# Softmax with a negated maximum and the scale moved out of the exponential, and the background modulation on VectorE alone, in a two-layer attention trunk

## The chip, the core and the metric

The kernel runs on one core of a Trainium2 chip. The metric is device time in microseconds (us), the median of several executions. The page of the profile and all queries below describe one execution on that core; their times count from the start of its span. Engines: PE multiplies matrices, PEld loads its weights, DVE is VectorE, ACT is ScalarE, POOL is GpSimd, SP issues the DMAs. Each engine works through its own queue in order, so an instruction that waits holds up all behind it on that engine.

## What is computed

512 latent tokens and 256 context tokens of width 2048 pass two layers. Each layer normalises its input, scales and shifts it with vectors made from a conditioning vector (the modulation), projects it, runs two kinds of attention, gates, projects back and adds. Cut to what matters:

```python
for l in range(2):
    mod  = silu(c)     @ w_mod[l] + b_mod[l]       # shift, scale, gate of the latents
    cmod = silu(c_ctx) @ w_mod[l] + b_mod[l]       # the same for the context
    h  = rmsnorm(x,  norm_g[l]) * (1 + scale)  + shift
    hc = rmsnorm(cx, norm_g[l]) * (1 + cscale) + cshift
    u, uc = h @ w_in, hc @ w_in
    # layer 0: A (8 heads) and B (8 heads);  layer 1: C (8 heads) and D (8 heads)
    y = concat(mixer1(u, uc), mixer2(u, uc)) * silu(ug)
    x = x + gate * (y @ w_o[l])                    # layer 0 does it for cx too

# A, differential:  p = softmax(q1 k1 / 8) - lam * softmax(q2 k2 / 8);  o = p v, then an RMS norm
# B, windowed:      p = softmax([s_ctx, s_window, sink])[..., :-1];      o = p v
# C and D:          p = softmax(scale * q k);                            o = p v
```

C has RMS-normalised queries and D low-rank ones, so the scale of a query row in C and D depends on the token.

## The kernel before, in words

**Precision.** Each fp32 operand of a matmul is split in a rounded high part and the rest, and a product is three matmuls (high by high, low by high, high by low). For each weight chunk ACT rounds (`wh`, L259) and DVE subtracts (`wl`, L218, a helper that all such subtractions share).

**Projections.** `proj` (L283) multiplies 16 chunks of the hidden state with one column block of weights, lines L278, L279 and L281, into PSUM banks `J`. ACT copies the result out: `r` for queries and keys (`roped`, L411 and L413, followed by the rotation with DVE L401 and L402 and POOL L403 and L404), `ev` for values (L447, L448).

**Attention.** For a block of 128 queries `scores` puts q k into the PSUM tile `S`, of which there is one. `softmax` (L484) takes on DVE the row maximum `mc` (L489), turns it into the bias `nb` (L492 with a sink, L494 without), on ACT the exponential `e` with its row sum `den` (L498), and on DVE the reciprocal `rd` (L503). The caller scales `e` by `rd` (L605 in B, L721 in C and D). In A the second map is multiplied by `r2` (L555) and added to the first times `r1` (L556). `p_transpose` transposes `e` on PE (L518) and splits it into `pth` (ACT L522) and `ptl` (DVE L218); `av` multiplies with the values (L533). In A and B the scale is an immediate number in the exponential and in `nb`; in C and D it is a column per query block, `qsc` or `dqs`, kept with both signs side by side (`both_signs`, L712).

**Modulation.** The shift and scale of layer 0 are made on PE at the start, up to about 170 us (`mod_first`). All others, 16 blocks of 512 columns, are made in the background by `mod_later` (L156): a block reads eight pieces of weights `mraw` (two buffers), and for each piece two rows `i` and the two vectors `v` (latents and context) it adds weight times a column of `silc` to `macc`. For `v = 0` DVE does multiply and add in one (L173). For `v = 1` ACT multiplies in place (L170) and POOL adds (L171). The last four blocks have `v = 0` alone.

**Order.** The program is one stream of instructions; the framework's scheduler sets each engine's order when it is built. `tick(n)` in the program counts up how many pieces of the modulation are due, so the pieces are handed over between heads: a few in A, most in B, the rest with the output projection. The stages by the time in the profile: layer 0's input up to about 220 us, A up to about 860, B up to 1370, output projection of layer 0 up to 1605, layer 1's input up to 1690, C up to 2140, D up to 2410, the end.

## Time and profile before

| what | value |
|---|---|
| median of 3 runs | 2575.29 us (2571.32 to 2575.84) |
| the profiled execution, its own time | 2573.45 us |
| its span in the profile | 2571.7 us |
| mean granted TensorE clock | 0.977 |
| PE busy | 2427.3 us, 94% |
| PEld busy | 2088.3 us, 81% |
| DVE busy | 1608.2 us, 63% |
| ACT busy | 1128.6 us, 44% |
| POOL busy | 517.6 us, 20% |

The profiled execution stands 0.07% under the median. A busy PE is not a PE at its peak, since matmuls are pipelined and their ends modelled; time that PE has lost shows as idle time in a stage and as a granted clock under 1.00. In a row of a window view the columns are the stretch, its length, the busy time of each engine with its instruction count, the granted clock, the busy share of the DMA engines and GB/s. In a row of a group they are line, engine, operation, tiles, shape and count, then busy us and mean ns, then the engine's idle time just before and what ended it. In a row of a timeline: start, duration, engine, line, operation, and in brackets idle time before it and what ended it.

### The profile page before, as it was taken

To read this page: it belongs to the slowest core of one execution; us is meant where nothing else is said; L and a number is where in the kernel's file an instruction comes from. 1 tells how busy PE (TensorE), PEld (TensorE's weight loads), DVE (VectorE), ACT (ScalarE), POOL (GpSimd) and SP (SyncE) were. 2 spreads that over 40 slices of the span, in tenths; PEclk is the share of its full clock that TensorE was granted. 3 is DMA by queue.
4 is the path that set the end of the run, shared out by engine and by line. 5 is a ranking of instruction groups with operands and counts; after the bars stand their busy time and mean duration, and the time that the engine had idled before them with its cause. 6 is when DMAs were issued, how large, how long until landed. Compare 5 with 4: busy or idle time off the path is not lost.

```text
span 2571.7 us, 36748 instructions
## 1 busy us (share of the span) xinstructions
PE 2427.3 (94%) x14214; PEld 2088.3 (81%) x14214; DVE 1608.2 (63%) x2720; ACT 1128.6 (44%) x2143; POOL 517.6 (20%) x340
## 2 busy tenths in 40 slices
PE   4889999999999999999999999899999999999998
PEld 2667888988788888878878888688888888887787
DVE  4367666656865787877666554857735325776534
ACT  3244444544554554544343332444434334554434
POOL 1132001101400354353303442310010001000010
PEclk9899999999999999999999999899999999999999
DMA  9762111111312233342334554535522222222234
GB/s 326 251 216 74 48 50 56 56 55 57 105 53 69 90 133 124 107 145 97 118 127 153 183 182 138 205 106 170 178 70 79 78 83 70 62 87 70 92 117 148
DMA packets 99087, 297.51 MB, mean 116 GB/s; under 512 B 11616, under 2 KB 12640, under 8 KB 98912
## 3 DMA queue, kind: packets, MB, share of 16 engines
q1 hardware_dynamic: 98912, 295.16, 34.5%
q8 instruction: 112, 1.84, 0.3%
q14 instruction: 63, 0.52, 0.1%
HBM read 269.16 MB, written 25.95 MB: 115 GB/s over the span
## 4 chain that ended last, share of the span: by engine, by line
PE 51%; DVE 7%; issue 2%; ACT 2%; DMA 2%; POOL 1%; ACTq 0%; SPq 0%; DVEq 0%; POOLq 0%
PE J L278 13%; PE J L279 13%; PE J L281 13%; PE O L533 4%; PE S L477 2%; DVE macc L173 2%; PE T L518 2%; DMA mraw<-in_wm_dram 2%; PE S L473 2%; DVE wl L218 1%; POOL macc L171 1%; DVE l L359 1%; DVE mc L489 1%; PE J L181 1%; PE T L243 0%
## 5 line engine op out<-in xcount | busy, mean ns | idle before, releaser
L278 PE MATMUL J<-h,wh 128*128 128x512 f32 (+1 forms) x2224 | 791.3, 359 | 23.8 <-ACT h L353 13.4
L279 PE MATMUL J<-l,wh 128*128 128x512 f32 (+1 forms) x2224 | 769.0, 356 | 4.7 <-DVE l L359 2.7
L281 PE MATMUL J<-h,wl 128*128 128x512 f32 (+1 forms) x2224 | 709.1, 356 | 2.8 <-DVE wl L218 2.8
L218 DVE TENSOR_TENSOR wl<-wraw,wh 128x512 fp32r<-128x512 f32 x500 | 402.2, 809 | 348.2 <-ACT wh L259 326.6
L259 ACT CAST wh<-wraw 128x512 fp32r<-128x512 f32 x492 | 302.4, 618 | 545.2 <-PE J L279 472.1
L278 PEld LDWEIGHTS J<-h,wh 128*128 128x128 f32 x2224 | 424.7, 192 | 104.7 <-ACT h L353 14.5
L279 PEld LDWEIGHTS J<-l,wh 128*128 128x128 f32 x2224 | 426.1, 192 | 62.6 <-DVE l L218 3.9
L281 PEld LDWEIGHTS J<-h,wl 128*128 128x128 f32 x2224 | 390.6, 192 | 38.8 <-DVE wl L218 5.1
L171 POOL TENSOR_TENSOR macc<-macc,mraw 128x512 f32<-128x512 f32 x180 | 267.9, 1489 | 254.1 <-ACT mraw L170 226.6
L278 PE MATMUL J<-yh,wh 128*128 128x512 f32 (+1 forms) x800 | 276.6, 352 | 5.1 <-ACT yh L441 5.1
L279 PE MATMUL J<-yl,wh 128*128 128x512 f32 (+1 forms) x800 | 272.8, 351 | 1.0 <-DVE yl L218 0.9
L173 DVE SCALAR_TENSOR_TENSOR macc<-mraw,silc,macc 128x512 f32<-128x512 f32 x240 | 241.7, 1007 | 42.3 <-DMA mraw<-in_wm_dram 38.6
L281 PE MATMUL J<-yh,wl 128*128 128x512 f32 (+1 forms) x800 | 253.2, 350 | 0.0
L489 DVE TENSOR_REDUCE mc<-S 128x1 f32<-128x768 f32 (+3 forms) x208 | 166.1, 799 | 137.9 <-PE S L477 88.1
L170 ACT ACTIVATE mraw<-mraw,silc 128x512 f32<-128x512 f32 x180 | 129.4, 723 | 192.4 <-DVE macc L173 171.6
L522 ACT CAST pth<-T 128x256 fp32r<-128x256 f32 (+2 forms) x288 | 124.9, 450 | 160.6 <-PE T L518 157.3
L278 PEld LDWEIGHTS J<-yh,wh 128*128 128x128 f32 x800 | 150.9, 190 | 32.8 <-ACT yh L441 5.9
L279 PEld LDWEIGHTS J<-yl,wh 128*128 128x128 f32 x800 | 151.1, 189 | 22.1 <-DVE yl L218 2.8
L218 DVE TENSOR_TENSOR ptl<-T,pth 128x256 fp32r<-128x256 f32 (+2 forms) x288 | 144.5, 514 | 38.6 <-ACT pth L522 35.1
L498 ACT ACTIVATE e<-S,nb 128x256 f32<-128x256 f32 (+3 forms) x144 | 104.3, 724 | 145.1 <-DVE nb L494 102.2
L281 PEld LDWEIGHTS J<-yh,wl 128*128 128x128 f32 x800 | 140.6, 190 | 12.4
L403 POOL TENSOR_TENSOR r<-r,cos 128x512 f32<-128x512 f32 x31 | 44.3, 1429 | 476.3 <-DVE t L402 361.4
(287 smaller groups left out, 3424.7 us busy)
## 6 DMA issues: line engine op xcount, KB each, us to landing
mraw<-in_wm_dram SPq DMA_DIRECT2D x128, 512.0 KB, 3.7
wraw<-in_ew_dram SPq DMA_DIRECT2D x96, 512.0 KB, 3.6
wraw<-in_ow_dram SPq DMA_DIRECT2D x64, 512.0 KB, 3.6
wraw<-in_wo_dram SPq DMA_DIRECT2D x62, 512.0 KB, 3.8
mraw<-in_wm_dram SPq DMA_DIRECT2D x80, 384.0 KB, 7.3
xT<-in_xT_dram SPq DMA_DIRECT2D x16, 384.0 KB, 7.8
res<-in_xT_dram SPq DMA_DIRECT2D x16, 384.0 KB, 4.4
xad<-nx SPq DMA_DIRECT2D x16, 384.0 KB, 2.3
```

Of the source, the lines that this page charges most:

```text
L170: nc.scalar.mul(rv[:, i, :], rv[:, i, :], sc)
L171: nc.gpsimd.tensor_tensor(macc[:, v, :], macc[:, v, :], rv[:, i, :], op=ALU.add)
L173: nc.vector.scalar_tensor_tensor(macc[:, v, :], rv[:, i, :], sc, macc[:, v, :], op0=ALU.mult, op1=ALU.add)
L218: nc.vector.tensor_tensor(o, a, h.bitcast(F32), op=ALU.subtract)
L259: nc.scalar.copy(wh[:, :n, :], rv[:, k0:k0 + n, :])
L278: nc.tensor.matmul(o, lhsT=wh, rhs=xh[:, c0:c1], start=first and (opens or o is lat), stop=False)
L279: nc.tensor.matmul(o, lhsT=wh, rhs=xl[:, c0:c1], start=False, stop=False)
L281: nc.tensor.matmul(o, lhsT=wl, rhs=xh[:, c0:c1], start=False, stop=last and (closes or o is lat))
L489: nc.vector.reduce_max(mc, S, axis=AX.X)
L498: nc.scalar.activation(e, S, AF.Exp, bias=nb, scale=scale, accum_out=den)
L522: nc.scalar.copy(ph, tv)
L533: nc.tensor.matmul(o, lhsT=v[:, cols[i]], rhs=pt[part][:, i, :], start=(n == 0), stop=(n == len(steps) - 1))
```

## The change

1. `softmax` lets the maximum come out negated (`tensor_reduce` with `negate=True`), so the multiplication by minus the scale goes. In A and B the scale is put into the queries where they leave PSUM (`roped`, L411 and L413: the copy becomes a multiplication), and the exponential's scale is 1. In C and D `nb` is multiplied by the scale column (`tensor_tensor`); with a sink, `nb` is the smaller of `nb` and `nsink` (`tensor_tensor` in place of `tensor_scalar`).
2. `both_signs` becomes `scaled`: one instruction in place of two, nine times.
3. The reciprocal moves out of `softmax` into `normed`. In A the first map is normed at once, before the second map's softmax; the second is then multiplied by `r2` and added to it in one instruction. The separate multiplication (L555) has gone from behind the second exponential.
4. In `mod_later` the branch for `v = 1` goes: 180 multiplications on ACT and 180 additions on POOL become 180 multiply-adds on DVE, as for `v = 0`.

```diff
@@ mod_later
                     if r == 0 and i == 0:
                         nc.scalar.mul(macc[:, v, :], rv[:, i, :], sc)
-                    elif v == 1:
-                        nc.scalar.mul(rv[:, i, :], rv[:, i, :], sc)
-                        nc.gpsimd.tensor_tensor(macc[:, v, :], macc[:, v, :], rv[:, i, :], op=ALU.add)
                     else:
                         nc.vector.scalar_tensor_tensor(macc[:, v, :], rv[:, i, :], sc, macc[:, v, :],
                                                        op0=ALU.mult, op1=ALU.add)
@@ roped
-    def roped(pl, pc, dim, mk=tmp):
+    def roped(pl, pc, dim, mk=tmp, scale=1.0):
         r = mk("r")
-        nc.scalar.copy(r[:, :512], pl)
+        nc.scalar.mul(r[:, :512], pl, scale)
...
@@ softmax
-    def softmax(S, scale, neg, sink=None):
+    def softmax(S, scale=None, sink=None):
         n = S.shape[-1]
-        mc = sm.tile([P, 1], F32, name="mc")
-        nc.vector.reduce_max(mc, S, axis=AX.X)
         nb = sm.tile([P, 1], F32, name="nb")
+        nc.vector.tensor_reduce(nb, S, axis=AX.X, op=ALU.max, negate=True)
+        if scale is not None:
+            nc.vector.tensor_tensor(nb, nb, scale, op=ALU.mult)
         if sink is not None:
-            nc.vector.tensor_scalar(nb, mc, neg, nsink[:, sink:sink + 1], op0=ALU.mult, op1=ALU.min)
-        else:
-            nc.vector.tensor_scalar(nb, mc, neg, None, op0=ALU.mult)
+            nc.vector.tensor_tensor(nb, nb, nsink[:, sink:sink + 1], op=ALU.min)
...
-        nc.scalar.activation(e, S, AF.Exp, bias=nb, scale=scale, accum_out=den)
+        nc.scalar.activation(e, S, AF.Exp, bias=nb, scale=1.0 if scale is None else scale, accum_out=den)
...
+        return e, den
+
+    def normed(e, den):
+        r = sm.tile([P, 1], F32, name="rd")
         nc.vector.reciprocal(r, den)
-        return e, r
+        nc.vector.tensor_scalar(e, e, r, None, op0=ALU.mult)
@@ a_attend
-                    e1, r1 = softmax(scores([(qa[:, c], k) for k in ka], lo, hi), 0.125, -0.125)
-                    e2, r2 = softmax(scores([(qb[:, c], k) for k in kb], lo, hi), 0.125, -0.125)
+                    e1, den = softmax(scores([(qa[:, c], k) for k in ka], lo, hi))
+                    normed(e1, den)
+                    e2, den = softmax(scores([(qb[:, c], k) for k in kb], lo, hi))
+                    r2 = sm.tile([P, 1], F32, name="rd")
+                    nc.vector.reciprocal(r2, den)
                     nc.vector.tensor_tensor(r2, r2, nlam, op=ALU.mult)
-                    nc.vector.tensor_scalar(e2, e2, r2, None, op0=ALU.mult)
-                    nc.vector.scalar_tensor_tensor(e1, e1, r1, e2, op0=ALU.mult, op1=ALU.add)
+                    nc.vector.scalar_tensor_tensor(e1, e2, r2, e1, op0=ALU.mult, op1=ALU.add)
@@ layer 1
-    def both_signs(cols, f):
...
+    def scaled(cols, f):
+        nc.vector.tensor_scalar(cols[:, :8], cols[:, :8], f, None, op0=ALU.mult)
```

In B and in C and D the callers do `e, den = softmax(...)` and `normed(e, den)` where they did the same work in one step before.

With the work, the scheduler's order moves on every engine. Lines of the changed kernel have other numbers (L170 is now the multiply-add, L486 the maximum, L490 the minimum with the sink, L497 the sum with the sink, L502 the reciprocal, L503 the scaling of `e`). Two places follow.

ACT, at the end of layer 0's input (190 to 215 us in the profile). Here `kh`, `qa`, `qb` and `vh` are rounded parts of A's first head, `th` is the gate, and `r` is the copy of the next head's key out of PSUM. Before:

```order
L433 CAST kh<-r 64x768 x2
L170 ACTIVATE mraw<-mraw,silc 128x512
L419 CAST qa<-r 64x768
L420 CAST qb<-r 64x768
L454 CAST vh<-J 128x512
L454 CAST vh<-J 128x256
L464 ACTIVATE th<-S 128x256
L170 ACTIVATE mraw<-mraw,silc 128x512
L411 COPY r<-J 128x512
```

And now:

```order
L430 CAST kh<-r 64x768 x2
L416 CAST qa<-r 64x768
L417 CAST qb<-r 64x768
L451 CAST vh<-J 128x512
L451 CAST vh<-J 128x256
L461 ACTIVATE th<-S 128x256
L408 ACTIVATE r<-J 128x512
```

The modulation's multiplications are gone from ACT's queue, and the copy `r`, which frees PE's bank, stands right behind `th`.

DVE, the first softmax of B (about 915 us in the profile); `ql` and `wl` are low parts of queries and weights. Before:

```order
L489 TENSOR_REDUCE mc<-S 128x1
L173 SCALAR_TENSOR_TENSOR macc<-mraw,silc,macc 128x512
L492 TENSOR_SCALAR nb<-mc,nsink 128x1
L173 SCALAR_TENSOR_TENSOR macc<-mraw,silc,macc 128x512
L502 TENSOR_TENSOR den<-den,es 128x1
L503 RECIPROCAL rd<-den 128x1
L605 TENSOR_SCALAR e<-e,rd 128x512
```

And now:

```order
L486 TENSOR_REDUCE nb<-S 128x1
L170 SCALAR_TENSOR_TENSOR macc<-mraw,silc,macc 128x512 x2
L490 TENSOR_TENSOR nb<-nb,nsink 128x1
L170 SCALAR_TENSOR_TENSOR macc<-mraw,silc,macc 128x512 x2
L215 TENSOR_TENSOR ql<-r,qh 128x768
L170 SCALAR_TENSOR_TENSOR macc<-mraw,silc,macc 128x512
L497 TENSOR_TENSOR den<-den,es 128x1
L170 SCALAR_TENSOR_TENSOR macc<-mraw,silc,macc 128x512
L215 TENSOR_TENSOR wl<-wraw,wh 128x512
L170 SCALAR_TENSOR_TENSOR macc<-mraw,silc,macc 128x512
L502 RECIPROCAL rd<-den 128x1
L170 SCALAR_TENSOR_TENSOR macc<-mraw,silc,macc 128x512 x2
```

Between the maximum and the scaled map stood two multiply-adds; nine stand there now (the scaling, L503, is the next row), and two subtractions.

More of the change, by code (lines that the diff above doesn't have):

```diff
@@ L407, in etile @@
         return sp["ep"].tile([P, TOK], F32, tag="e", name=name)
-    def roped(pl, pc, dim, mk=tmp):
+    def roped(pl, pc, dim, mk=tmp, scale=1.0):
         r = mk("r")
-        nc.scalar.copy(r[:, :512], pl)
+        nc.scalar.mul(r[:, :512], pl, scale)
         if pc is not None:
-            nc.scalar.copy(r[:, 512:768], pc)
+            nc.scalar.mul(r[:, 512:768], pc, scale)
         rope(r, dim)
@@ L579, in trunk_kernel @@
         tick(.4 if h else 0)
-        r = roped(*first(1, A_Q0), 64, mk)
+        r = roped(*first(1, A_Q0), 64, mk, 0.125)
         qa, qb = q_stacks(r, TOK, slotr)
@@ L603, in b_attend @@
             for u, h in enumerate(pr):
-                e, rd = softmax(scores(passes3(*qs[u], kh, kl, t), lo, hi, masks), SC128, -SC128, sink=h)
-                nc.vector.tensor_scalar(e, e, rd, None, op0=ALU.mult)
+                e, den = softmax(scores(passes3(*qs[u], kh, kl, t), lo, hi, masks), sink=h)
+                normed(e, den)
                 p_transpose(e, pt, u)
@@ L627, in trunk_kernel @@
             for h in pr:
-                r = roped(*proj(w, B_Q0 + 128 * h), 128)
+                r = roped(*proj(w, B_Q0 + 128 * h), 128, scale=SC128)
                 qs.append(split(r, TOK, slotr, "q"))
@@ L706, in trunk_kernel @@
             mm_step(lat, cx, ws4[i][k % 4], hT[k], k == 0, k == NCH - 1, opens=(i % 2 == 0), closes=(i % 2 == 1))
-    def both_signs(cols, f):
-        v = cols[:, :8].rearrange("p (t s) -> p t s", s=2)
-        for i, g in ((0, f), (1, -f)):
-            nc.vector.tensor_scalar(v[:, :, i], v[:, :, i], g, None, op0=ALU.mult)
+    def scaled(cols, f):
+        nc.vector.tensor_scalar(cols[:, :8], cols[:, :8], f, None, op0=ALU.mult)
     def full_attend(kfn, vh, vl, scale_of, sg=None):
@@ L719, in full_attend @@
                 t = 2 * pi + u
-                e, rd = softmax(scores(kfn(t), 0, 4), *scale_of(t))
-                nc.vector.tensor_scalar(e, e, rd, None, op0=ALU.mult)
+                e, den = softmax(scores(kfn(t), 0, 4), scale_of(t))
+                normed(e, den)
                 p_transpose(e, pt, u)
@@ L765, in d_lowrank @@
         cols = rstd_cols((acc,), range(4), 512, "dqs", tbank)
-        both_signs(cols, SC192)
+        scaled(cols, SC192)
         dqs.append(cols)
@@ L797, in trunk_kernel @@
             qsc = rstd_cols((sq,), range(4), P, "qsc", tbank)
-            both_signs(qsc, SC128)
+            scaled(qsc, SC128)
             rope(ev, 128)
@@ L801, in trunk_kernel @@
             o = full_attend(lambda t: passes3(qh, ql, kh, kl, t), vh, vl,
-                            lambda t: (qsc[:, 2 * t:2 * t + 1], qsc[:, 2 * t + 1:2 * t + 2]))
+                            lambda t: qsc[:, 2 * t:2 * t + 1])
             sg = silu2(*proj(w, O_G0 + 128 * h, lat_only=True), sgslot)
@@ L891, in trunk_kernel @@
             nc.sync.dma_start(sg[:, :512], sgd[h])
-            o = full_attend(passes, *vs[u], lambda t: (dqs[0][:, 2 * t:2 * t + 1], dqs[0][:, 2 * t + 1:2 * t + 2]), sg)
+            o = full_attend(passes, *vs[u], lambda t: dqs[0][:, 2 * t:2 * t + 1], sg)
             if h < 6:
```

1 line of the change is left out of this document (removed).

## The prediction

> **What bounds the kernel now.** I read the page's busy times, a table by stage, the list of waits, and the timeline where PE stood longest.
>
> ```profile
> PE 2427.3 (94%) x14214; PEld 2088.3 (81%) x14214; DVE 1608.2 (63%) x2720; ACT 1128.6 (44%) x2143; POOL 517.6 (20%) x340
> ```
>
> ```profile
> 150.00:220.00 70.00, 56.19 (x349) 43.92 (x348) 59.36 (x66) 35.90 (x58) 32.00 (x20) 0.93 0.45 144
> 220.00:640.00 420.00, 412.58 (x2538) 367.46 (x2537) 260.64 (x522) 199.50 (x383) 34.85 (x24) 1.00 0.16 54
> 640.00:700.00 60.00, 53.72 (x318) 47.53 (x317) 53.83 (x74) 33.54 (x58) 29.06 (x19) 0.94 0.35 115
> ...
> 860.00:1290.00 430.00, 403.65 (x2467) 357.57 (x2466) 325.82 (x490) 209.06 (x457) 196.09 (x130) 0.98 0.38 121
> ...
> 1370.00:1605.00 235.00, 235.00 (x1376) 207.37 (x1375) 138.67 (x158) 79.68 (x121) 93.81 (x59) 1.00 0.51 171
> ...
> 2140.00:2410.00 270.00, 256.24 (x1524) 218.65 (x1522) 188.03 (x362) 133.51 (x269) 14.47 (x11) 0.99 0.22 69
> ```
>
> PE bounds. What it loses in a stage is its idle time plus the share of the clock not granted. The two-vector modulation runs in four stretches: 150 to 220 loses 13.8 + 0.07 x 70 = 18.7 us, 640 to 700 loses 6.3 + 3.6 = 9.9, 860 to 1290 loses 26.4 + 8.6 = 35.0, and 1370 to 1605 nothing. Together that is 63.6 us. The same attention A without it, 220 to 640, loses 7.4 us in 420. So the modulation's neighbourhood is where PE starves, though no engine is full there: in 860 to 1290 DVE is busy 76%. A queue in order is one reason:
>
> ```profile
> ACT mraw L170 <- DVE macc L173: 171.6, 109, 4.7
> ...
> DVE macc L173 <- DMA mraw<-in_wm_dram: 38.6, 35, 3.1
> ```
>
> ```profile
> 1110.15 0.52 PE L281 MATMUL J<-h,wl 128*128 128x512 f32 x2
> 1111.63 1.75 DVE L173 SCALAR_TENSOR_TENSOR macc<-mraw,silc,macc 128x512 f32<-128x512 f32 x2 [0.71 <-DMA mraw<-in_wm_dram]
> ...
> 1112.68 1.46 ACT L170 ACTIVATE mraw<-mraw,silc 128x512 f32<-128x512 f32 x2 [2.70 <-DVE macc L173]
> ...
> 1114.87 0.59 ACT L447 COPY ev<-J 128x512 f32<-128x512 f32 x1
> ...
> 1115.52 0.90 PE L453 MATMUL J<-identr,ev 128*128 128x128 f32 x3 [4.85 <-ACT ev L447]
> ```
>
> ACT multiplies in place, so it waits until DVE has read the row; ACT stands 2.70 us behind DVE, which stood behind a DMA, and the copy `ev` that PE needs is queued behind ACT's multiplications. PE stands 4.85 us. The second reason is POOL. While it adds (first row), DVE's instructions take longer; after 691 they don't:
>
> ```profile
> 675.66 4.50 POOL L171 TENSOR_TENSOR macc<-macc,mraw 128x512 f32<-128x512 f32 x3
> ```
>
> ```profile
> 675.65 1.85 DVE L173 SCALAR_TENSOR_TENSOR macc<-mraw,silc,macc 128x512 f32<-128x512 f32 x1
> 677.43 1.62 DVE L555 TENSOR_SCALAR e<-e,rd 128x768 f32<-128x768 f32 x1
> 678.96 1.75 DVE L173 SCALAR_TENSOR_TENSOR macc<-mraw,silc,macc 128x512 f32<-128x512 f32 x1
> ...
> 691.16 0.16 DVE L554 TENSOR_TENSOR rd<-rd,nlam 128x1 f32<-128x1 f32 x1
> 691.35 0.62 DVE L555 TENSOR_SCALAR e<-e,rd 128x768 f32<-128x768 f32 x1
> ```
>
> ```profile
> 682.56 1.54 PE L518 MATMUL T<-identr,e 128*128 128x128 f32 x6 [5.20 <-DVE e L556]
> ```
>
> **The change part by part: DVE's load.** L173 alone, by stage, then POOL's L171 in 860 to 1290:
>
> ```profile
> 860.00:1290.00 430.00, 114.72 (x105) 0.98 0.38 121
> ...
> 1690.00:2140.00 450.00, 33.57 (x45) 1.00 0.33 107
> ```
>
> ```profile
> 860.00:1290.00 430.00, 155.38 (x105) 0.98 0.38 121
> ```
>
> Beside POOL's additions a multiply-add takes 114.72 / 105 = 1.093 us, without them 33.57 / 45 = 0.746. The 105 that move in this stage therefore cost 78 us, and the 105 already there give back 36. The rest gives back too; groups of 860 to 1290:
>
> ```profile
> L218 DVE TENSOR_TENSOR wl<-wraw,wh 128x512 fp32r<-128x512 f32 x72 | 76.1, 1062 | 38.5 <-ACT wh L259 33.6 <-PE J L281 3.7 <-PE J L279 0.6
> L605 DVE TENSOR_SCALAR e<-e,rd 128x512 f32<-128x512 f32 (+2 forms) x36 | 27.8, 774 | 0.9
> ...
> L502 DVE TENSOR_TENSOR den<-den,es 128x1 f32<-128x1 f32 x36 | 15.0, 417 | 14.0 <-ACT es L501 13.9
> ...
> L492 DVE TENSOR_SCALAR nb<-mc,nsink 128x1 f32<-128x1 f32 x36 | 7.5, 208 | 0.6
> ```
>
> L502 is L554's kind, 0.16 us when clean: 36 x 0.26 = 9. For `wl`, 0.746 is an upper bound (less work than a multiply-add): 72 x 0.32 = 23. L605 is at most 0.62 when clean (the longer L555): at least 36 x 0.15 = 6. That is 74 of 78 us, so DVE stays about as busy as now (bounds: +42 us if only L173 gains, -10 if the remaining small rows gain likewise), while ACT loses 180 instructions and POOL its 180 additions. I take zero net, nearest to the rows.
>
> **What PE gets back.** What ended its idle time in 860 to 1290, by group:
>
> ```profile
> L518 PE MATMUL T<-identr,e 128*128 128x128 f32 x144 | 23.4, 285 | 9.1 <-DVE e L605 9.1
> ...
> L473 PE MATMUL S<-kh,qh 128*128 128x256 f32 x36 | 11.4, 315 | 7.0 <-ACT e L498 3.4 <-ACT qh L441 3.3
> ...
> L453 PE MATMUL J<-identr,ev 128*128 128x128 f32 x12 | 2.4, 356 | 5.0 <-ACT ev L447 5.0
> ```
>
> Without L170 the copy `ev` starts at about 1112: 3 us of the 5.0. Of the 9.1 and 7.0 I take half, 8 us, since these waits hold both inflated DVE rows, which go, and multiply-adds queued ahead, which grow. Of the clock's 8.6 us half goes with the long stops: 4.3. With 0.9 behind POOL's last addition that is 16 us of 35.0; bounds are 4 (`ev` and the addition alone) and 35. In 640 to 700 the three DVE rows beside POOL's addition are 1.10 + 1.00 + 1.00 = 3.1 us too long, just before a stop of 5.20: 3 us, and half of the clock's 3.6, so 5 (bounds 0 and 9.9). In 150 to 220:
>
> ```profile
> 205.98 0.40 ACT L464 ACTIVATE th<-S 128x256 f32<-128x256 f32 x1
> 209.27 0.72 ACT L170 ACTIVATE mraw<-mraw,silc 128x512 f32<-128x512 f32 x1 [2.89 <-DVE macc L173]
> ```
>
> ```profile
> 210.52 0.58 PE L278 MATMUL J<-h,wh 128*128 128x256 f32 x1 [5.71 <-ACT r L411]
> ```
>
> The copy `r` now follows `th` at 206.4, not L170 at 209.9: 3.5 us, and 1.5 of the clock. Against it, 15 more multiply-adds, 11 us, stand between the subtractions for the last four hidden chunks; the 15 already there give back 4.8. I charge 2 us. Net 3 (bounds -4 and 18.7). In 1370 to 1605 PE is full: zero, covered by 96 us of idle DVE. SP issues the same DMAs; its `mraw` loads, with weight loads behind them, now wait for DVE alone. Landing takes 3.7 us and a piece 4 x 0.746 = 3.0 on DVE, so with two buffers DVE can wait 0.7 us or more per piece: zero if other rows stand between, 96 x 0.7 = 67 us if none do. I leave the 38.6 us as they are.
>
> ```profile
> mraw<-in_wm_dram SPq DMA_DIRECT2D x128, 512.0 KB, 3.7
> ```
>
> **The softmax edits.**
>
> ```profile
> L494 DVE TENSOR_SCALAR nb<-mc 128x1 f32<-128x1 f32 x96 | 14.2, 148 | 1.7
> ...
> L494 DVE TENSOR_SCALAR nb<-mc,dqs 128x1 f32<-128x1 f32 x32 | 6.6, 206 | 0.3
> ```
>
> A loses 96 x 0.148 = 14.2 us of DVE and gets the multiplication of the second map off the end of its chain; the cover is PE's queue of projections, full in 220 to 640, so 1 us shows (bounds 0 and 7.4). In D (2140 to 2410, PE idle 13.8) the 206 ns become a `tensor_tensor`, 0.16 when clean: 32 x 0.05 = 1.5, of which 1. A negating maximum I price as the old one; its price isn't in the trace, between zero and the 0.148 that it replaces. The nine fewer `scaled` rows, and ACT's copies turned into multiplications, are off the path: zero. B swaps the form of `nb`. The Trainium skill, "SBUF — State Buffer", "Who interferes with whom", says that a VectorE instruction with two inputs in SBUF contends with a GpSimd one that reads SBUF, and one with a single SBUF input outside the two-port modes does not. L502's 417 ns against L554's 0.16 us agrees. By that rule alone the new `nb` would pay L502's 0.26 us, 36 x 0.26 = 9 us, on the chain; with POOL busy 196.09 - 155.38 = 41 us there in place of 196, it is 2, about what the 208 ns of L492 give back.
>
> **The sum.** 16 + 5 + 3 + 2 = 26 us against the profiled execution's own 2573.45: 2547.4. That execution lies 1.8 us under the median of the runs, so I predict 2549.
>
> **Rivals.** (a) All the lost time in the four stretches returns, as in A without modulation: 63.6 less 2% of 795 us of stretches (16) and plus 2 is 50, so 2525; if nothing at all were lost there, 2510. For it: ACT's and POOL's share in every long stop. Against it: DVE's 76%. (b) The change doesn't do what it says: DVE's queue takes the place of ACT's, stops move but stay, 2573 within 5. The Trainium skill, "Perfetto Trace Analysis", "Optimizing Scalar/DVE Operations", says that work moved between GpSimd and VectorE might not help since they share a port; the slow rows agree on the sharing. (c) Slower: in B the multiply-adds lengthen the chain from maximum to scaled map. In the order quoted there are nine where two stood, 7 x 0.746 = 5.2 us more against about 1.2 us of inflation gone (2 x 0.35, 0.26, 0.15). Now PE waits (9.1 + 7.0) / 36 = 0.45 us per softmax. If that grows by 1 us, 36 us come on and only `ev`, the clock and the other stretches, about 16, go: 2595. It decides from about 0.45 us more per softmax. Against it: the same rows are DVE work that PE's projections cover today.
>
> **Chances.** The forecast 0.58, with its own range 2532 to 2564; (a) 0.15; (b) 0.12; (c) 0.15. About 0.2%, 5 us, is what a measurement can tell from no change. Faster takes the forecast, (a) and a quarter of (b): 0.76; same the rest of (b): 0.09; slower (c): 0.15. The range 2515 to 2583 leaves out part of (a) and most of (c).
>
> **What would show it.** The multiply-add (then L170) at about 0.75 us in every stage; no wait of ACT for it; ACT near 1128.6 - 180 x 0.73 = 997 us busy and POOL near 517.6 - 180 x 1.48 = 251, DVE within 40 of 1608; PE's loss in B (860 to 1290) near 19 us. Wrong: waits of PE for the scaled `e` or of ACT for `nb` in B above 16 us, or DVE waiting for `mraw` well over 38.6.

## The result: 2515.59 us, 0.9774 of the time before

| kernel | median | ratio to before, 95% interval |
|---|---|---|
| before | 2574.18 us (2571.32 to 2575.84, 4 runs) | 1 |
| after | 2515.59 us (2510.88 to 2520.86, 4 runs) | 0.9774 [0.9752, 0.9796] |

The change gains 58.6 us, where 26 were forecast: the direction is right, the time lies at the very lower end of the range 2515 to 2583 and below the forecast's own range 2532 to 2564, and the forecast gain is less than half of what came. The profiled execution of after has a span of 2508.9 us, 62.8 less than before's. The page's busy times, after:

```profile
PE 2408.6 (96%) x14214; PEld 2077.9 (83%) x14214; DVE 1574.6 (63%) x2795; ACT 1011.5 (40%) x1963; POOL 248.9 (10%) x160
```

PE is busy 18.7 us less for the same matmuls (they run at a higher granted clock, 0.985 for 0.977), and the other 44 us are idle time gone. DVE does the additions that POOL did, with 75 instructions more, and yet is busy 33.6 us less. The table by stage shows where PE's time came back. These are the stretches of the prediction, moved to where the same work lies in after; first the profile of after, then attention B alone (from its first query product to the first product of the output projection) in before:

```profile
150.00:208.00 58.00, 51.51 (x323) 40.19 (x323) 51.95 (x77) 24.95 (x42) 6.69 (x4) 0.94 0.46 157
640.00:700.00 60.00, 59.75 (x367) 53.07 (x366) 53.76 (x83) 26.93 (x51) 6.01 (x4) 1.00 0.32 106
889.00:1237.00 348.00, 345.83 (x2182) 311.28 (x2181) 271.24 (x536) 126.69 (x324) 36.50 (x22) 1.00 0.40 131
1310.00:1546.00 236.00, 236.00 (x1382) 208.35 (x1381) 137.33 (x203) 50.45 (x77) 27.00 (x14) 1.00 0.50 170
2140.00:2335.00 195.00, 189.94 (x1160) 163.08 (x1159) 140.91 (x282) 100.27 (x205) 8.01 (x6) 1.00 0.23 73
```

```profile
913.00:1293.00 380.00, 356.67 (x2176) 316.33 (x2175) 283.28 (x445) 184.81 (x414) 168.04 (x112) 0.97 0.38 121
```

B takes 348 us for 380. PE's loss there (idle time plus the clock's share) goes from 23.3 + 0.03 x 380 = 34.7 us to 2.2, while DVE is as full as before: 271 of 348 is 78%, 283 of 380 was 75%. DVE does 91 instructions more in B in 12 us less, because most of them are shorter. Groups of B in after (889 to 1237):

```profile
L170 DVE SCALAR_TENSOR_TENSOR macc<-mraw,silc,macc 128x512 f32<-128x512 f32 x180 | 133.3, 775 | 3.3 <-DMA mraw<-in_wm_dram 2.9 <-ACT macc L168 0.2
L215 DVE TENSOR_TENSOR wl<-wraw,wh 128x512 fp32r<-128x512 f32 x64 | 45.0, 703 | 34.6 <-ACT wh L256 33.3 <-PE J L278 1.0
...
L497 DVE TENSOR_TENSOR den<-den,es 128x1 f32<-128x1 f32 x36 | 5.6, 157 | 14.1 <-ACT es L496 14.1
```

The multiply-add is 0.74 us of busy time (133.3 / 180) where it was 1.09, `wl` 0.70 where it was 1.06, and the sum of two columns `den` 0.157 where it was 0.417.

Stages in us, each from one profiled execution, by landmarks in PE's rows: the start up to A's first query product; A; B up to the first product of the output projection; that projection (with B's last attention in it); layer 1's input; C; D up to its last query product. The last column is the median. The kernels are told below:

| kernel | start | A | B | out | input 1 | C | D | median |
|---|---|---|---|---|---|---|---|---|
| before | 216 | 697 | 380 | 313 | 85 | 506 | 200 | 2574 |
| mod_only | 212 | 695 | 350 | 312 | 85 | 506 | 200 | 2537 |
| act_dve | 206 | 695 | 350 | 312 | 89 | 505 | 201 | 2534 |
| pool_ts | 203 | 706 | 443 | 315 | 83 | 507 | 200 | 2633 |
| softmax_only | 216 | 690 | 388 | 310 | 91 | 505 | 195 | 2568 |
| after | 208 | 681 | 348 | 309 | 88 | 506 | 195 | 2516 |
| late_norm | 205 | 685 | 348 | 313 | 85 | 506 | 195 | 2513 |
| extra_nb | 206 | 689 | 348 | 310 | 89 | 505 | 195 | 2518 |
| both_back | 209 | 695 | 347 | 312 | 87 | 505 | 195 | 2526 |
| junk_b | 208 | 684 | 351 | 313 | 88 | 507 | 196 | 2522 |
| junk_b2 | 207 | 683 | 383 | 325 | 87 | 508 | 195 | 2564 |
| junk_b4 | 210 | 683 | 434 | 331 | 85 | 506 | 196 | 2618 |
| xn_dve | 209 | 684 | 348 | 311 | 75 | 507 | 195 | 2500 |
| after_rev | 208 | 686 | 347 | 310 | 88 | 505 | 196 | 2516 |
| all_dve | 215 | 684 | 347 | 309 | 77 | 505 | 199 | 2513 |

Between kernels that are alike there, the start varies by 5 us (205 to 210), input 1 by 8 (83 to 91 in all but xn_dve and all_dve) and A by 5 (681 to 686 in the six kernels that have after's A).

### The profile page after: what moved, and what is told of

The parts are those of the page before. It is cut to its first block, busy times and chain, and to the rows that moved or that the text cites. A ratio compares the mean times of both kernels' runs of the same rounds, so it can differ in the third digit from the quotient of the medians.

```text
span 2508.9 us, 36275 instructions
## 1 busy us (share of the span) xinstructions
PE 2408.6 (96%) x14214; PEld 2077.9 (83%) x14214; DVE 1574.6 (63%) x2795; ACT 1011.5 (40%) x1963; POOL 248.9 (10%) x160
## 3 DMA queue, kind: packets, MB, share of 16 engines
q1 hardware_dynamic: 98912, 295.16, 34.7%
## 4 chain that ended last, share of the span: by engine, by line
PE 88%; DVE 5%; DMA 3%; issue 2%; ACT 1%; SPq 0%; ACTq 0%; DVEq 0%
PE J L275 22%; PE J L276 22%; PE J L278 22%; PE O L532 6%; PE S L474 4%; PE T L517 3%; PE S L470 3%; DMA mraw<-in_wm_dram 2%; DVE macc L170 1%; PE T L144 1%; PE J L178 1%; DVE l L356 1%; DVE wl L215 1%; PE T L240 1%; PE T L220 1%
## 5 line engine op out<-in xcount | busy, mean ns | idle before, releaser
L275 PE MATMUL J<-h,wh 128*128 128x512 f32 (+1 forms) x2224 | 786.0, 357 | 18.7 <-ACT h L350 11.8
L215 DVE TENSOR_TENSOR wl<-wraw,wh 128x512 fp32r<-128x512 f32 x500 | 362.6, 729 | 338.7 <-ACT wh L256 325.2
L170 DVE SCALAR_TENSOR_TENSOR macc<-mraw,silc,macc 128x512 f32<-128x512 f32 x420 | 319.7, 792 | 28.6 <-DMA mraw<-in_wm_dram 26.2
L486 DVE TENSOR_REDUCE nb<-S 128x1 f32<-128x768 f32 (+3 forms) x208 | 166.2, 799 | 146.8 <-PE S L474 79.2
L517 PE MATMUL T<-identr,e 128*128 128x128 f32 x784 | 115.5, 274 | 2.9 <-DVE e L503 2.6
L517 PEld LDWEIGHTS T<-identr,e 128*128 128x128 f32 x784 | 94.6, 141 | 16.6 <-issue 2.6
```

Of the source, the lines that this page charges most:

```text
L170: nc.vector.scalar_tensor_tensor(macc[:, v, :], rv[:, i, :], sc, macc[:, v, :], op0=ALU.mult, op1=ALU.add)
L215: nc.vector.tensor_tensor(o, a, h.bitcast(F32), op=ALU.subtract)
L275: nc.tensor.matmul(o, lhsT=wh, rhs=xh[:, c0:c1], start=first and (opens or o is lat), stop=False)
L486: nc.vector.tensor_reduce(nb, S, axis=AX.X, op=ALU.max, negate=True)
L517: nc.tensor.transpose(out=tp[:, 128 * (b - b0):128 * (b - b0) + 128], in_=e[:, 128 * b:128 * b + 128], identity=ident)
```

## The experiments

Two theories stood at the start. P: POOL's additions lengthen DVE's instructions, through something that the two engines share, and DVE's instructions stand on the chain that PE waits for. Q: ACT, waiting in its queue for DVE's reads, holds up the copies and exponentials that PE needs.

### One part of the change each

**mod_only** is before with the branch of the second vector deleted, nothing else of the change:

```diff
-                    elif v == 1:
-                        nc.scalar.mul(rv[:, i, :], rv[:, i, :], sc)
-                        nc.gpsimd.tensor_tensor(macc[:, v, :], macc[:, v, :], rv[:, i, :], op=ALU.add)
```

> The kernel before with the modulation's v = 1 on VectorE and nothing else changed. Theory M (all of the gain comes from the modulation leaving ACT and POOL): about 2520 us, 54 less than before, and PE loses almost nothing from 860 to 1235 us. Theory S (the softmax edits bring a third or more, since chains with fewer steps hide the multiply-adds): about 2540 us, and B still loses 15 us. Theory O (the scheduler's new order was lucky, and no single part carries it): anywhere from 2530 to 2580.

Measured: 2537.17 us, 0.9856 [0.9841, 0.9871], 36.4 us gained.

**softmax_only** is after with these three lines put back.

> The changed kernel with the modulation put back on ACT and POOL as before. Theory M: 2570 us, within 6 of before, and B loses about 35 us as before. Theory S: 2550 us or less. Theory O: anywhere from 2540 to 2590.

Measured: 2568.46 us, 0.9978 [0.9966, 0.9991], 5.1 us gained. The parts alone give 36.4 + 5.1 = 41.5 of 58.6 us; behind the modulation's move the softmax edits give 2537.17 - 2515.59 = 21.6. The table shows where the 17 us more that come together lie: beside POOL's additions the new softmax makes B 8 us longer (388 for 380) and A 7 shorter, without them B 2 shorter and A 14. Groups by form, whole kernel, first softmax_only, then after:

```profile
L493 DVE TENSOR_TENSOR nb<-nb,nsink 128x1 f32<-128x1 f32 x48 | 18.3, 382 | 0.8
```

```profile
L490 DVE TENSOR_TENSOR nb<-nb,nsink 128x1 f32<-128x1 f32 x48 | 10.1, 211 | 0.7
```

The new form of `nb`, a `tensor_tensor` of two columns, takes 382 ns in a kernel with POOL's additions, for the 208 of the old form: 48 x 0.174 = 8.4 us, all on the chain between maximum and exponential. The prediction had 9 us for this price and saw it go with the additions; it did. The longest row of the old form in before is 0.216 us, that of the new form in softmax_only 1.248. The Trainium skill, "SBUF — State Buffer", "Who interferes with whom", names two SBUF inputs as what makes a VectorE instruction contend with a GpSimd one that reads SBUF, and excepts an instruction with one such input outside the two-port modes. By that rule the old form, if it ran in no such mode, would stay short and the new would not, and both rows agree. One input alone is no safe sign: the scaling of `e` has one tile as input too, and took 1.62 us for 0.62 in the rows of the prediction.

### P against Q

**act_dve** is before with POOL's additions on DVE; ACT still multiplies in place, and still waits:

```diff
-                        nc.gpsimd.tensor_tensor(macc[:, v, :], macc[:, v, :], rv[:, i, :], op=ALU.add)
+                        nc.vector.tensor_tensor(macc[:, v, :], macc[:, v, :], rv[:, i, :], op=ALU.add)
```

> The kernel before, with POOL's additions of the modulation moved to VectorE, while ACT still multiplies in place and so still waits for VectorE's reading. No POOL work beside it any more. Theory P (the shared reading port was the main cost): 2530 us, and a multiply-add takes 0.75 us. Theory Q (ACT's queue was the main cost, since the copies that PE needs stand behind multiplications that wait): 2560 us, with ACT's wait for the multiply-add still near 170 us and PE stopped behind ACT's copies.

Measured: 2534.28 us, 0.9841 [0.9826, 0.9856], 39.3 us gained. From the waits of ACT in act_dve, and its row for B:

```profile
ACT mraw L170 <- DVE macc L173: 134.5, 102, 4.2
```

```profile
901.00:1251.00 350.00, 345.41 (x2175) 310.27 (x2173) 271.69 (x535) 185.76 (x414) 36.36 (x22) 1.00 0.40 130
```

ACT does all its 180 multiplications and waits 134.5 us for DVE (171.6 in before), yet B is as short as in mod_only (350). PE's wait for the copy `ev`, 4.8 us of B in before, is not among its waits in B any more.

**pool_ts** is before with ACT's multiplications on POOL, so that ACT is free of the modulation and POOL does both steps:

```diff
-                        nc.scalar.mul(rv[:, i, :], rv[:, i, :], sc)
+                        nc.gpsimd.tensor_scalar(rv[:, i, :], rv[:, i, :], sc, None, op0=ALU.mult)
```

> The kernel before, with ACT's multiplication of the modulation moved to POOL (a tensor_scalar in place), so ACT is out of it and POOL has 360 instructions in place of 180. Theory Q: 2535 us, since no copy stands behind a waiting multiplication. Theory P: 2575 us or more, since POOL holds the port for longer and a multiply-add stays at 1.1 us or above in B.

Measured: 2633.18 us, 1.0228 [1.0211, 1.0245], 59.6 us lost. The row for B and the group of POOL's multiplications in pool_ts:

```profile
909.00:1352.00 443.00, 370.56 (x2193) 327.81 (x2191) 278.46 (x454) 129.54 (x328) 343.62 (x215) 0.90 0.34 109
```

```profile
L170 POOL TENSOR_SCALAR mraw<-mraw,silc 128x512 f32<-128x512 f32 x180 | 338.4, 1889 | 155.7 <-DVE macc L173 118.5 <-DVE nb L494 22.7 <-DVE modc L129 9.6
```

ACT has what Q wanted for it, and B grows by 63 us. Not all of that is sharing. POOL is busy 344 of 443 us in B, and PE waits 25.5 us for the modulation itself, which now comes late (in all, number of times, longest):

```profile
PE J L181 <- DVE macc L173: 25.5, 5, 10.7
```

So pool_ts shows that freeing ACT doesn't pay for more work on POOL, but not how much of the loss is the slowing of DVE. Q as the main cost falls by act_dve: ACT's wait was there, and in single places PE stood behind it, but the gain comes with 134.5 of its 171.6 us still there.

### POOL's additions with nobody waiting for them

Deleting POOL's additions also takes a dependence away. So they were given back to after as work that no one needs.

**junk_pool** adds four 128x128 additions into a scratch tile beside each multiply-add of the second vector:

```diff
+                        for _ in range(4 * v):
+                            nc.gpsimd.tensor_tensor(junk, junk, ones, op=ALU.add)
```

> The kernel after, with work added that nobody needs or waits for: beside each of VectorE's multiply-adds for the second vector, GpSimd makes four 128x128 additions of two SBUF tiles into a scratch tile of its own (672 instructions in all, about the elements of the additions that the change took away). Results are unchanged. Theory P (GpSimd's additions cost by slowing VectorE's instructions through what the two share): the multiply-adds go from 0.79 us towards 1.1 on average, the time rises by 25 to 55 us, 2540 to 2570, most of it in attention B. Rival R (what cost was the dependence between engines: additions that wait for ScalarE and buffers that are held for them): nobody depends on these, so within 5 us of the kernel after, 2513 to 2521.

Measured: 2579.93 us, 1.0026 [1.0018, 1.0035], 64 us slower than after, but not as meant. The view by tile of the scratch tile:

```profile
L175 POOL TENSOR_TENSOR junk<-junk,ones x720: 447/461/1259, 1.7 to 522.3; 128x128 f32<-128x128 f32 x180
```

(duration in ns least, median, greatest; first and last start in us.) Since they wait for nothing, all 720 (four for each of 180 multiply-adds) run ahead, between 2 and 522 us, and POOL's own work for the start and for A stands behind them in its queue: the start takes 239 us for 208 and A 719 for 681, B is unchanged at 347. This doesn't tell sharing from queueing.

**junk_b** puts small additions behind B's maxima, so that they lie in B (`nb` gets 16 buffers here and in the next two kernels, so that POOL's reading holds none back):

```diff
+            for _ in range(10):
+                nc.gpsimd.tensor_tensor(junk, junk, nb.broadcast_to([P, 96]), op=ALU.add)
```

> The kernel after, with GpSimd additions that nobody needs in attention B alone: ten 128x96 additions into a scratch tile behind each of B's 48 softmaxes (480 in all, some 190 us of GpSimd; they wait for VectorE's negated maximum, so they are spread over the stage, and nothing waits for them but GpSimd's own later work). Results are unchanged. In the run with additions that wait for nothing, all of them ran ahead, in the start and in A, where GpSimd was full and the rotary work stood behind them; here they lie where the kernel before had its additions. B loses 2.7 us in the kernel after and 35.5 in the kernel before. Theory P (sharing alone): multiply-adds and wl of B get 0.2 to 0.4 us longer, B's loss rises by 15 to 40 us, 2531 to 2556; A and D stay. Rival R (it was the queues and the buffers held): within 5 us of the kernel after, 2511 to 2521.

Measured: 2521.65 us, 0.98 [0.9784, 0.9816], 6.1 slower than after. Its row for B:

```profile
892.00:1243.00 351.00, 346.25 (x2175) 310.54 (x2173) 289.53 (x534) 125.42 (x324) 228.84 (x382) 1.00 0.39 130
```

POOL is busy 192 us more than in after, but DVE only 18, and B is 3 us longer. The expectation missed: an addition 96 wide with a single column as one input slows DVE little. Whether the width or the column is the reason wasn't told apart.

**junk_b2** and **junk_b4** use the full form on a scratch tile of 128x512, two or four times behind each of B's 48 softmaxes:

```diff
+            nc.gpsimd.tensor_tensor(junk[:, 0:1], junk[:, 0:1], nb, op=ALU.add)
+            for _ in range(2):       # junk_b4: 4
+                nc.gpsimd.tensor_tensor(junk, junk, cs["cos"], op=ALU.add)    # 128x512
```

> The kernel after, with two full GpSimd additions (128x512, both inputs in SBUF, about 1.45 us each) into a scratch tile behind each of B's 48 softmaxes: 96 additions, some 140 us, where the kernel before had 105 in this stage, 155 us. Nothing waits for them but GpSimd's own later work; they and ScalarE's tiles have no buffer in common. Results are unchanged. Theory P (sharing alone): the multiply-adds beside them take 1.1 to 1.5 us, B's loss goes from 2.7 us to 20 to 45, 2533 to 2558. Rival R (queues and held buffers were the cost): 2511 to 2521.

> The same with four full additions behind each softmax, 192 in all, some 280 us: GpSimd nearly full in B. Theory P: the loss more than doubles against the two-addition kernel, since VectorE then has no room left (271 us busy of 348 in the kernel after): 2570 to 2610, part of it the rotary sums that stand behind the additions in GpSimd's queue. Rival R: below 2530.

Measured: junk_b2 2563.91 us, 0.9957 [0.9944, 0.997], 48.3 slower than after; junk_b4 2617.88, 1.0173 [1.0158, 1.0189], 102.3 slower. That is 0.50 and 0.53 us per addition. In junk_b2, B is 35 us longer than in after, and the stage behind it, which holds B's last attention, 16. The rows for B, first junk_b2, then junk_b4:

```profile
890.00:1273.00 383.00, 358.56 (x2180) 315.40 (x2179) 331.83 (x535) 125.20 (x324) 158.46 (x130) 0.99 0.37 119
```

```profile
893.00:1327.00 434.00, 380.72 (x2178) 333.06 (x2178) 385.03 (x536) 126.75 (x324) 274.33 (x202) 0.93 0.33 105
```

With 158 us of POOL in B (before: 168) the 535 DVE instructions of the stage (536 in after) take 332 us for 271, and B is 383 us long, as in before (380). Nothing waits for the additions but POOL's own later work, and ACT has no part in them. Nor is it another order: by the tiles that they write and read, all 14214 matmuls of junk_b2 and all DVE instructions stand in after's sequence. So P is shown for B: in after's order, POOL's additions lengthen DVE's rows and cost 35 us; what it is that the two engines share, no trace shows. How it looks on the engines, in the timeline of junk_b2, POOL's rows and two of DVE's (DVE's rows between are left out):

```profile
908.47 4.00 POOL L497 TENSOR_TENSOR sqA<-sqA,cos 128x512 f32<-128x512 f32 x2
```

```profile
909.53 1.78 DVE L170 SCALAR_TENSOR_TENSOR macc<-mraw,silc,macc 128x512 f32<-128x512 f32 x1
911.23 1.25 DVE L500 TENSOR_TENSOR den<-den,es 128x1 f32<-128x1 f32 x1
...
912.74 0.74 DVE L170 SCALAR_TENSOR_TENSOR macc<-mraw,silc,macc 128x512 f32<-128x512 f32 x1
```

While POOL's two additions last (to 912.47) a sum of two 128x1 columns takes 1.25 us, eight times the mean of 0.157 in after, and the multiply-add 1.78; behind them the multiply-add is back at 0.74. Over B `den` takes, and the scaling of `e`, in junk_b2:

```profile
L500 DVE TENSOR_TENSOR den<-den,es 128x1 f32<-128x1 f32 x36 | 27.9, 775 | 14.1 <-ACT es L499 14.1
...
L506 DVE TENSOR_SCALAR e<-e,rd 128x640 f32<-128x640 f32 x12 | 12.2, 1015 | 0.2
```

These two stand between the exponential and the transposes. What PE waits for in B of junk_b2 (in all, times, longest):

```profile
PE O L535 <- DVE ptl L215: 8.4, 10, 2.1
PE T L520 <- DVE e L506: 7.5, 8, 2.2
```

In after neither is among PE's waits in B. For the rotated queries, which stand behind the additions in POOL's queue, PE waits 2.0 us in junk_b2 (0.3 for `qh`, 1.7 for `ql`), so POOL's queue is not the cause.

The chain did not get shorter with the change. In the traces, for the first 36 of B's 48 softmaxes, these are the means from the start of the maximum to the end of the scaled map, and to PE's first transpose of that map:

| kernel | to the scaled map | to PE's transpose | spare time |
|---|---|---|---|
| before | 5.06 us | 6.54 us | 1.48 us |
| softmax_only | 5.19 | 6.66 | 1.47 |
| act_dve | 5.20 | 8.12 | 2.93 |
| mod_only | 6.47 | 9.59 | 3.12 |
| after | 6.26 | 9.74 | 3.48 |
| junk_b2 | 7.89 | 9.03 | 1.14 |

With nine multiply-adds where two stood, the chain is 1.2 us longer in after than in before, as rival (c) had feared, though most rows are shorter. PE comes 3.2 us later for the map, and not because it waits: between a block's last score and its first transpose it does 68 other matmuls in the mean in after and junk_b2, 50 in before. The scheduler set PE's order anew with the work on DVE. In junk_b2, with after's order, POOL's additions alone lengthen the chain by another 1.6 us and use up most of the spare time. So that they cost is shown; how much of the 32 us between before and after is the shorter rows themselves, and how much the order that goes with the change, is not separated.

### The softmax edits, taken apart

In A and D they gain what the prediction gave as 2 us. Stops of PE in the timeline (start, duration, in brackets PE's idle time and what ended it), in before one in A and one in D, then in mod_only one in A:

```profile
286.30 0.39 PE L473 MATMUL S<-kh,qb 128*128 128x256 f32 x1 [4.62 <-ACT e L498]
...
2243.84 0.58 PE L473 MATMUL S<-kh,qh 128*128 128x256 f32 x1 [3.27 <-ACT e L498]
```

```profile
376.72 0.58 PE L470 MATMUL S<-kh,qb 128*128 128x256 f32 x1 [4.63 <-ACT e L495]
```

Each is PE waiting to refill the one tile `S` until the exponential has read it. After has no such stop of over 1 us in A or D; in D, 200 us become 195 (idle time 8.3 to 5.1, clock 0.98 to 1.00, by the row of after above and this one of before).

```profile
2197.00:2397.00 200.00, 191.66 (x1156) 164.56 (x1155) 142.94 (x282) 100.28 (x203) 8.00 (x6) 0.98 0.23 71
```

**late_norm** is after with A's first map scaled last again, as before:

```diff
-                    normed(e1, den)
+                    r1 = sm.tile([P, 1], F32, name="rd")
+                    nc.vector.reciprocal(r1, den)
...
-                    nc.vector.scalar_tensor_tensor(e1, e2, r2, e1, op0=ALU.mult, op1=ALU.add)
+                    nc.vector.tensor_scalar(e2, e2, r2, None, op0=ALU.mult)
+                    nc.vector.scalar_tensor_tensor(e1, e1, r1, e2, op0=ALU.mult, op1=ALU.add)
```

> The kernel after, with one edit undone: in attention A the first map is again scaled last (the second map times r2, then the first map times r1 plus the second), so that its end has two 768-wide VectorE instructions instead of one. All other edits stay. A loses 12.2 us of TensorE in the kernel after and 25.7 with the modulation move alone. Theory N (it is the earlier normalization that shortened A's chain): A goes back to 23 to 26 us lost, 2527 to 2530 us. Theory M (it is the negated maximum and the scale in the queries, 96 small VectorE instructions fewer): A stays at 12 to 15 us, 2516 to 2519. If each takes half: about 2522.

Measured: 2513.26 us, 0.9772 [0.9757, 0.9786]: no loss. A is 685 us, 4 more than after's and within what A varies by.

**extra_nb** puts one 128x1 instruction back into each of A's 96 softmaxes:

```diff
+        if scale is None and sink is None:
+            nc.vector.tensor_scalar(nb, nb, 1.0, None, op0=ALU.mult)
```

> The kernel after, with one VectorE instruction put back into each of A's 96 softmaxes: the negated maximum is multiplied by 1.0 on its way to the exponential (128x1, about 0.15 us each, 14 us of VectorE in all). The normalization of the first map stays early. Theory M (the 96 small instructions on the chain between maximum and exponential are what A's gain of 9 to 13 us came from): A loses 21 to 26 us again, 2524 to 2530. Rival S (A's gain is in which few places TensorE's order leaves a stop, not in 0.15 us a softmax): within 5 us of the kernel after, 2511 to 2521.

Measured: 2518.42 us, 0.9792 [0.9776, 0.9808], 2.8 more than after, within its uncertainty. A is 689.

**both_back** has both of these edits.

> The kernel after, with both edits of A's chain undone at once: the negated maximum multiplied by 1.0 on its way (0.15 us), and the first map scaled last, as before. The kernels with A unchanged lose 12 to 17 us there (four of them), with the first alone 20.4, with the second alone 17.0; with the modulation move alone A loses 25.7. If the two add up: 22 to 23 us lost in A, 2520 to 2525. If one covers for the other, so that only both together bring the stops back: 25 us or more, 2525 to 2532. If what is left is the order alone: 15 to 18, 2514 to 2520.

Measured: 2525.85 us, 0.9812 [0.9798, 0.9827], 10.3 more than after. A is 695, as in mod_only. The same stop in both_back, then in extra_nb:

```profile
375.14 0.54 PE L470 MATMUL S<-kh,qb 128*128 128x256 f32 x1 [4.63 <-ACT e L495]
```

```profile
369.45 0.38 PE L470 MATMUL S<-kh,qb 128*128 128x256 f32 x1 [1.76 <-ACT e L495]
```

With both edits undone the stop stands again at its full 4.63 us; with the small instruction alone it is 1.76, with the late scaling alone it is not there. So A's gain is not 0.15 us a softmax summed up, but a few stops, which are back in full only where both edits are undone. Whether they went with the shorter chain or with the order is not settled: PE's sequence in A differs between after, late_norm and extra_nb, while both_back has mod_only's (4136 of 4137 matmuls of A in one sequence, by their tiles). The 14 us between mod_only's A and after's hold 5.9 us of PE's wait for `e` at `S` (none in after), the wait for `ev` (4.2 us, then 0.9) and a lower clock behind the stop: 0.78 and 0.88 in the 20 us from 370 on in mod_only, 1.00 there in after.

### The order as a cause

**after_rev** takes the two vectors in reversed sequence, in the kernel after:

```diff
-                for v in range(nv):
+                for v in reversed(range(nv)):
```

> The same control on the kernel after: the second vector's multiply-add ahead of the first vector's, nothing else. If the time hangs on what the engines have to do, within 6 us of the kernel after, 2510 to 2522. If the kernel after is a lucky order, it goes back by 10 us or more, towards 2530.

Measured: 2516.1 us, 0.9784 [0.9767, 0.9801], 0.5 from after. This says nothing of the order: by the tiles, all 14214 matmuls of after_rev stand in after's sequence, so for PE it is no other order. Against a lucky order in B speak other runs: mod_only, act_dve and after have three different sequences of PE in B, none has POOL's additions, and B takes 350, 350 and 348 us; junk_b2 has after's sequence and the additions, and B takes 383.

**before_rev** is the same line in the kernel before. In it the first vector's sums read rows that ScalarE has already multiplied for the second, so that its modulation has other values.

> A control for the order. The kernel before with the two vectors of each modulation step in reversed sequence (the second vector, ScalarE's and GpSimd's, ahead of the first): the same instructions with the same durations, but an order on the engines that the program's scheduler settles anew. If the time hangs on what the engines have to do, within 6 us of the kernel before, 2567 to 2579. If single places of the order decide, it can move by 10 to 30 us to either side.

Measured: 2612.03 us, 1.0154 [1.0137, 1.017]. It is no control, since the edit changed a dependence too: DVE's multiply-add now waits for ACT's multiplication. Its group in before_rev:

```profile
L173 DVE SCALAR_TENSOR_TENSOR macc<-mraw,silc,macc 128x512 f32<-128x512 f32 x240 | 285.8, 1191 | 44.1 <-ACT mraw L170 20.1 <-DMA mraw<-in_wm_dram 14.4 <-ACT macc L168 2.8
```

The mean goes from 1007 ns (241.7 us for 240 in before) to 1191; this was not followed further.

### Further on the same road

**xn_dve** moves ten normalizing multiplications of layer 1's input from POOL to DVE:

```diff
-        (nc.gpsimd if k % 3 else nc.vector).tensor_tensor(xn, xk, rs, op=ALU.mult)
+        (nc.gpsimd if k % 3 and l == 0 else nc.vector).tensor_tensor(xn, xk, rs, op=ALU.mult)
```

> The kernel after, with layer 1's ten normalizing multiplications `xn` that run on GpSimd (2.24 us each) moved to VectorE (0.95 us each). TensorE loses 27 us in this stage, more than in any other after the start. Theory P says that VectorE's rows beside it get shorter and that ScalarE's `h` gets its input sooner: 5 to 10 us gained, 2506 to 2511. Rival D (VectorE is what paces this stage, busy 67 of 88 us, and gets 9.5 us more): no gain or a loss, 2516 to 2522.

Measured: 2500.35 us, 0.9718 [0.9702, 0.9734], the fastest of all. Layer 1's input, its row by stage and then the group of `l` in this stretch, first of after, then of xn_dve:

```profile
1546.00:1634.00 88.00, 74.94 (x354) 62.07 (x353) 67.03 (x88) 34.64 (x64) 29.20 (x14) 0.84 0.54 187
```

```profile
L356 DVE SCALAR_TENSOR_TENSOR l<-xn,modc,h 128x512 fp32r<-128x512 f32 (+1 forms) x32 | 31.2, 1023 | 0.8 <-ACT h L350 0.8
```

```profile
1552.00:1627.00 75.00, 68.50 (x351) 58.60 (x350) 60.65 (x98) 33.66 (x64) 5.90 (x4) 0.89 0.64 219
```

```profile
L356 DVE SCALAR_TENSOR_TENSOR l<-xn,modc,h 128x512 fp32r<-128x512 f32 (+1 forms) x32 | 18.2, 607 | 0.0
```

DVE takes ten instructions of 0.95 us more and is busy 6.4 us less, since `l` loses 13.0 us; the stage is 13 us shorter. Two other things changed with it and were not separated: `xn` itself is made in 0.95 us for 2.24, and DVE's wait for `mraw` in this stage goes from 7.0 to 1.9 us.

**all_dve** moves every `tensor_tensor` of POOL to DVE (`nc.gpsimd` becomes `nc.vector` in `make_h`, `rope`, `finish` and the three sums of squares).

> The kernel after, with every tensor_tensor of GpSimd (140 of them: the rotary products and sums, the gated outputs, the sums of squares, the normalizing multiplications, 249 us in all) on VectorE, so that GpSimd does nothing. VectorE gets about 140 x 0.85 = 119 us and loses what is left of its slowdown (the multiply-adds at 0.79 against 0.75, wl at 0.73 against 0.69: some 40 to 60 us in all). Theory P in its plain form (GpSimd beside VectorE costs more than it brings, everywhere): 2500 to 2510. Rival D (work leaves GpSimd only with a gain where VectorE's slowed rows stand on TensorE's path; elsewhere it only makes VectorE's queue longer): 2513 to 2530.

Measured: 2512.61 us, 0.9767 [0.975, 0.9783]: 3 us under after, within their uncertainty, and 12 us more than xn_dve. It keeps most of the gain in input 1 (77 us) and loses in the start (215 for 208) and in D (199 for 195), where DVE's queue grows; that no slowed row of weight is won back there is the likely reason, not a tested one.

## Why the prediction was wrong, point by point

The modulation's move was put at 24 us and the softmax edits at 2. Alone, the move gave 36.4 (mod_only); behind it, the softmax edits gave 21.6. Taken in the other order the softmax edits gave 5.1 and the move 53.5. So two terms of the sum were too small, and they are not independent.

- **What PE gets back in B, 16 us: the step that failed.** It took half of the waits 9.1 and 7.0 for the scaled `e` and for ACT, 3 of the 5.0 for `ev`, the 0.9 behind POOL's last addition and half of the clock's 8.6 us. B got 32 us shorter, and its loss fell by 34.7 - 2.2 = 32.5; mod_only and act_dve have 30 us of it each, and junk_b2 loses 35. The halves were a guess between bounds of 4 and 35, held down by "multiply-adds queued ahead, which grow". They did grow, and the chain with them, 5.06 to 6.26 us; but the step set them against PE's order of before, and what PE does meanwhile grew more: PE comes for the map 9.74 us after the maximum starts, for 6.54, and waits 2.2 us in all. The slowing beside POOL, which takes most of that time in junk_b2, went nearly altogether and not by half.
- **The same in 640 to 700 and 150 to 220.** 5 and 3 us were taken. In 640 to 700 PE's loss is 0.25 us where it was 9.9. In 150 to 208 it is 6.5 + 0.06 x 58 = 10.0 for 18.7.
- **ACT's queue as the first reason: wrong.** The row at 1109 to 1116 was read rightly as a stop behind ACT, but act_dve keeps ACT's multiplications and 134.5 us of its wait, gains 39.3 us and has no wait of PE for `ev` in B. The second reason, POOL's additions, was the one that counted.
- **DVE's load, zero net: right.** In B 283 became 271 us; over the span DVE is 33.6 us less busy, inside the 40 named. So are POOL's 248.9 us (251 named), the multiply-add (0.74 us in B), and DVE's wait for `mraw`, 26.2 us, not above 38.6. ACT's 1011.5 are 14 us above the 997 named.
- **1370 to 1605, zero: right.** PE was and is full there (236.00 of 236).
- **The softmax edits, 2 us: wrong by a factor of ten** behind the modulation's move (21.6), and near with POOL's additions in place (5.1). This is the second step that failed, and by the size of the miss as large as the first. It priced instructions (32 x 0.05, 1 us shown of 14.2) and took PE's projections as cover. The trace held stops of 4.62 us in A and 3.27 us in D with the exponential's reading of `S` at their end, on the chain that these edits shorten; neither was set against the edit. They are not there in after; in A it is open whether the shorter chain or the new order removed them. The bound of 7.4 us for A looked at 220 to 640 alone; A as a whole went from 697 to 681.
- **A sign of being wrong that could not tell.** Waits "of ACT for `nb` in B above 16 us" were to speak against the forecast. They were 33.8 us before the change, and are 54.4 in B of after (in all, times, longest), while PE loses almost nothing:

```profile
ACT e L498 <- DVE nb L492: 33.8, 17, 4.9
```

```profile
ACT e L493 <- DVE nb L490: 54.4, 21, 8.7
```

- **The rivals.** (a), all the lost time of the four stretches returns, 2525 down to 2510, had 0.15, and its time is what came. It was held down by "DVE's 76%", and that share turned out to say nothing. Part of the hit is luck: the stretches gave 32.5 + 9.7 + 8.7 = 50.9 us, and the rest came from the other parts of A and from D, where (a) had 2 us; without the softmax edits the time was 2537. (b) and the sentence beside it did not come true: work moved from GpSimd to VectorE gained 36.4 us. The Trainium skill, "Perfetto Trace Analysis", "Optimizing Scalar/DVE Operations", says only that it might not help; here the measurement decides, and the slowing beside POOL, which agrees with the sharing that the page gives as its reason, is what the move took away. (c) had its premise right: the chain in B grew by 1.2 us, more than the 0.45 from which it was to decide. Its conclusion did not follow, since PE's order gave the chain more time: no wait of PE for the scaled `e` in B is left among its waits there.

## What to carry to other kernels

Where POOL adds tiles in SBUF beside a busy DVE, look at the durations of DVE's rows in and out of POOL's intervals, the small two-input ones first: if a 128x1 sum takes several times its own length, what POOL saves DVE it may take from the chain, and here work went to a DVE at 76% with a gain. Neither DVE's busy share nor the number of rows on the chain tells what such a move costs; compare the length of the chain with the time that PE's own order leaves for it, and expect the scheduler to change that order with the work. Ten instructions gave 15 us here, all 140 with these among them 3, which is within the uncertainty. For an edit that shortens a chain, look for the stops that end in that chain: here the gain was in whole stops, not in the sum of the instructions saved. And before a reordered kernel is taken as a control, compare the order on the engine that bounds.

## What was not expected of the hardware

- A DVE sum of two 128x1 columns took up to 1.25 us beside a POOL addition of 128x512 and 0.157 in the mean of after. In the rows shown it grew by 1.09 us and the 128x512 multiply-add by 1.04: the price did not go by the instruction's own size.
- POOL's busy time did not tell the cost: in B, 192 us of additions 96 wide with one column as input cost 3 us, 122 us of 128x512 additions cost 35. Width, input and number differ between the two, and were not told apart.
- A row maximum that negates its result costs what the plain one does, so that in A the instruction behind it is saved in full. Groups by form, before and then after:

```profile
L489 DVE TENSOR_REDUCE mc<-S 128x1 f32<-128x768 f32 x128 | 122.0, 953 | 89.3 <-PE S L477 88.1
```

```profile
L486 DVE TENSOR_REDUCE nb<-S 128x1 f32<-128x768 f32 x128 | 122.1, 954 | 80.3 <-PE S L474 79.2
```
